# A per-channel gate moved from a projection's weights to its results, and one branch's additions moved to VectorE

## The chip, the cores and the metric

The kernel runs on one core of one Trainium2 chip. The metric is device time in microseconds (us) of one execution; several executions are summarised by their median. TensorE does the matrix products into PSUM (8 banks of 128x512 float32), VectorE (DVE), ScalarE (ACT) and GpSimd (POOL) do the elementwise work, and SyncE (SP) issues nearly all DMAs. Each engine works through its own instructions in the order of its queue, and waits at the head of the queue for whatever the next instruction needs.

## What is computed

A decoder block on a sequence of 1024 rows with 1024 channels. An S5 branch and a stick-breaking attention branch are merged by sigmoid gates, projected by `w_o`, scaled by a modulation row `g1` and added to the input; a SwiGLU feed-forward part follows.

```python
y_a = s5_branch(...) @ w_a
y_b = stick_breaking_attention(q, k, v) @ w_b
merged = (sigmoid(gate_a) * y_a + sigmoid(gate_b) * y_b) @ w_o
x = x + g1 * merged                                  # g1: one value for each of 1024 channels
h = modulate(rmsnorm(x, norm2_g), sh2, sc2)
ffn = (silu(h @ w_ffn_gate) * (h @ w_ffn_up)) @ w_ffn_down
x = x + g2 * ffn
return rmsnorm(x, norm_f_g)
```

## The kernel before

Every float32 matrix operand is split into a high part (a copy rounded to the type `F32R`, on ScalarE) and a low part (the difference, on VectorE), and each product is made of three matmuls (`PRODUCTS`: high by high, high by low, low by high). A matmul here is 128x128 by 128x512. The stages follow one another; three of them matter.

`branch_b` (L954) is the attention branch's projection and the merge. Four groups of output channels (`c`), two blocks `m` in each and two halves `h` of the sequence make 16 results. For each: the pre-activation of the gate (`gt`) and the S5 side (`ma`) are loaded by SP (L975, L976), ScalarE takes the sigmoid (L977), TensorE makes 12 matmuls into one PSUM bank (L982), VectorE multiplies the bank by `gt` (L984), which frees the bank, then `ma` is added (L985: on VectorE for `h` = 1, on GpSimd for `h` = 0), and `split` makes the high part on ScalarE (L904) and the low part on VectorE (L905). `gt` and `ma` have six buffers each, so the loads of a later result wait for an earlier one to be split. Between the groups, `ada_row` builds `g1` as a row repeated on all partitions (L886 writes it), and `ada_cols` builds two small columns.

`attend_out` (L1000) is the output projection, the residual and the norm. `c` counts two halves of the output channels. For each half, four weight tiles of 128x1024 come through `weight` (L404): load by SP (L411), times `g1` on GpSimd (L416), high part on ScalarE (L418), low part on VectorE (L421). For each block of 128 rows `t` (8 of them), 24 matmuls (L1018) fill a bank of the pool `wo`, and VectorE adds it to the row tile `x1[t]` (L1021). In the second half (`c` = 1) the finished row goes on: to DRAM (L1024), squared with a sum on ScalarE (L1030), the reciprocal root in seven small instructions (`rstd`, L449 to L460), scaled into the tile `xh` (L1032), and, for each odd `t`, two rows' `xh` are transposed on TensorE into four banks `tq` (L1040) and moved out by ScalarE (L1046, even `kk`) and VectorE (L1044, odd `kk`). `xh` is a tile of a pool `ot` with 3 buffers, except for `t` = 3 and 7, where it is the one buffer `row` of another pool. That buffer is the one that `g1` lies in: `g1` is last read by L416.

`ffn` (L1054) begins with `pieces` (L990), sums and splits of the transposed rows (L437, L439, L440), of which seven sets are needed before `gate_up`'s matmuls (L1137) can run without a break. The first two sets need rows 0 to 511 only (`t` up to 3); the others need all rows.

PSUM is handed over between `branch_b` and `attend_out`: the 16 results of `branch_b` go round 8 banks, and the three banks of `wo` are banks 1, 2 and 3. The 15th result of `branch_b` lies in bank 1 and the 16th in bank 2.

What sets the order: except for some pinned places, the order of the instructions in each engine's queue is written out by a scheduler ahead of time, from a model of the time that each takes; on the chip the order is fixed. A tile's buffer is given to its next user when all readers of the old tile are done.

Of the kernel before, what the change touches and what calls it, by code (L numbers as in the profile page):

```python
# [9 lines left out]
F32 = mybir.dt.float32  # L10
# [3 lines left out]
ALU = mybir.AluOpType  # L14
# [320 lines left out]
P = 128  # L335
# [56 lines left out]
class Block:  # L392
# [8 lines left out]
        return self.tc.tile_pool(name=name, bufs=bufs, space=space)  # L401


    def weight(self, src, scale=None, lo_eng=None, hi_eng=None, first=None, ring=None):  # L404

        nc = self.nc
        pool, ht, lt, spool, stag, sbufs = ring or self.next_ring()
        st = spool.tile([P, 1024], F32, name=stag, bufs=sbufs)
        h = pool.tile([P, 1024], F32R, name=ht)
        l = pool.tile([P, 1024], F32R, name=lt)  # L410
        ld = nc.sync.dma_start(out=st.rearrange("p (a b) -> p a b", b=src.shape[-1]) if len(src.shape) == 3 else st, in_=src)  # L411
        if first is not None:
            self.after(ld, first)
        if scale is not None:
            sv = st.rearrange("p (a b) -> p a b", b=src.shape[-1]) if len(src.shape) == 3 else st
            nc.gpsimd.tensor_tensor(sv, sv, scale, ALU.mult)  # L416
        if hi_eng is None:
            nc.scalar.copy(h, st)  # L418
        else:
            hi_eng.tensor_scalar(h, st, 1.0, 0.0, ALU.mult, ALU.add)  # L420
        (lo_eng or nc.vector).tensor_tensor(l, st, h.bitcast(F32), ALU.subtract)  # L421
        return h, l
# [531 lines left out]
    def branch_b(self, ops, const, tp, pa, spare, g1):  # L954
        nc, i = self.nc, self.i
# [3 lines left out]
        for c in range(4):  # L959
# [7 lines left out]
            for m in (2 * c, 2 * c + 1):  # L967
                wm = [t[:, :, P * (m % 2):P * (m % 2) + P] for t in w]
                for h in range(2):
                    s = slice(512 * h, 512 * h + 512)  # L970
                    if spare:
                        gt, ma = spare.pop(0)
                    else:
                        gt, ma = (tp.tile([P, 512], F32, name=n, bufs=6) for n in ("gb", "ma"))
                    nc.sync.dma_start(out=gt, in_=self.gD[1, P * m:P * m + P, s])  # L975
                    nc.sync.dma_start(out=ma, in_=self.nD[P * m:P * m + P, s])  # L976
                    self.after(nc.scalar.activation(gt, gt, AF.Sigmoid), self.last_exp)  # L977
                    ps = pa.tile([P, 512], F32)
                    j = 0
                    for k in range(4):  # L980
                        for a, b in PRODUCTS:
                            nc.tensor.matmul(ps, lhsT=wm[a][:, k], rhs=ops[k][b][:, s], start=(j == 0), stop=(j == 11))  # L982
                            j += 1
                    nc.vector.tensor_tensor(gt, ps, gt, ALU.mult)  # L984
                    (nc.vector if h else nc.gpsimd).tensor_tensor(gt, gt, ma, ALU.add)  # L985
                    self.split(mg[h][m][:, 0], mg[h][m][:, 1], gt)
        return mg

# [11 lines left out]
    def attend_out(self, mg, g1, const, tp, pp, tpp):  # L1000
# [4 lines left out]
        x1, xhs = [], []  # L1005
        for c in range(2):
            cs = slice(512 * c, 512 * c + 512)
            gc = g1[:, cs].unsqueeze(1).broadcast_to([P, 2, 512])
            ws = [self.w3(self.weight(src[:, 2 * a:2 * a + 2, cs], scale=gc), 512) for a in range(4)]
            for t in range(KT if c == 0 else 0):  # L1010
                x1.append(self.X.tile([P, 1024], F32, name="x1"))
                nc.sync.dma_start(out=x1[t], in_=x_v[:, t])
            for t in range(KT):
                ps = pp.tile([P, 512], F32, name="wo")
                j = 0
                for k in range(KT):
                    for a, b in PRODUCTS:
                        nc.tensor.matmul(ps, lhsT=mg[t // 4][k][:, a, P * (t % 4):P * (t % 4) + P], rhs=ws[k // 2][b][:, k % 2],  # L1018
                                         start=(j == 0), stop=(j == 23))
                        j += 1  # L1020
                nc.vector.tensor_tensor(x1[t][:, cs], ps, x1[t][:, cs], ALU.add)  # L1021
                if c == 0:
                    continue
                nc.sync.dma_start(out=self.xD[P * t:P * t + P], in_=x1[t])  # L1024
                if t % 4 == 0:
                    f = [[self.F.tile([P, 2, 512], F32, name=f"f{y}") for _ in range(2)] for y in range(2)]
                xh = self.rp.tile([P, 1024], F32, name="row") if t % 4 == 3 else tp.tile([P, 1024], F32, name="xh")
                xhs.append(xh)
                ss = const.tile([P, 1], F32, name="ss2", bufs=2)
                nc.scalar.activation(xh, x1[t], AF.Square, accum_out=ss)  # L1030
# [388 lines left out]
```

## Time and profile before

| | |
|---|---|
| median of 3 runs | 1570.67 us (1568.31 to 1572.18) |
| the profiled execution | 1567.69 us |
| its span, first to last instruction | 1566.0 us |
| TensorE busy | 1420.6 us (91%) |
| VectorE busy | 1076.0 us (69%) |
| GpSimd busy | 820.9 us (52%) |
| ScalarE busy | 615.5 us (39%) |
| mean granted TensorE clock | 0.965 |

The profile shows each instruction with its start and duration, and in brackets the idle time of its engine just before it and what ended that idle time. "issue" is idle time for which the profile shows no wait. The chain of waits is followed back from the end: each piece is the work that released the next one. The granted clock is a share of 2.4 GHz: 1.00 is that level and 0.50 is 1.2 GHz. A busy share is not a limit by itself; where it matters is which engine or wait ends last in a stage.

### The profile page before, as it was taken

Reading aid. Unit: us, or ns where it says so; the run is one execution under the profiler, and the core shown is the slowest. Engines: PE = TensorE matmul, PEld = TensorE weight load, DVE = VectorE, ACT = ScalarE, POOL = GpSimd, SP = SyncE. Lnnn points to the kernel's source line nnn. Section 1 sums busy time; section 2 is a strip of 40 time slices with the busy share of each in tenths; the row PEclk is TensorE's granted clock in tenths of the full one; section 3 lists DMA queues with packets and bytes.
Section 4 is the critical chain, followed back from the end, with each engine's and each line's share of the span. In section 5 each row is a group of like instructions: output and inputs, shape, how many; then the busy total and the mean of one; then the engine's idle time right before and its main releaser. Section 6 shows DMA issues by size and latency. Waiting matters only on the chain.

```text
span 1566.0 us, 18381 instructions
## 1 busy us (share of the span) xinstructions
PE 1420.6 (91%) x6578; PEld 1113.9 (71%) x6578; DVE 1076.0 (69%) x1309; ACT 615.5 (39%) x792; POOL 820.9 (52%) x643
## 2 busy tenths in 40 slices
PE   4898889799999889888799879999999998999995
PEld 2697767678765556556688668888888887788774
DVE  5548777543567687775733797666665667999998
ACT  5431111352465656564314643332223332443323
POOL 2488694010345455632430445544555469797795
PEclk9899999999999999999899989999999999999998
DMA  8456675635423233326443413333333238445422
GB/s 284 160 139 180 178 194 172 178 117 160 142 96 115 70 107 115 108 88 203 133 162 119 125 53 101 101 101 107 110 108 109 72 128 303 149 154 148 121 60 108
DMA packets 180451, 210.46 MB, mean 134 GB/s; under 512 B 28612, under 2 KB 121896, under 8 KB 180360
## 3 DMA queue, kind: packets, MB, share of 16 engines
q1 hardware_dynamic: 169288, 201.29, 40.8%
q10 hardware_dynamic: 11072, 8.00, 1.8%
q8 instruction: 52, 0.85, 0.2%
q14 instruction: 39, 0.32, 0.1%
HBM read 159.18 MB, written 48.89 MB: 133 GB/s over the span
## 4 chain that ended last, share of the span: by engine, by line
PE 26%; DVE 10%; issue 7%; POOL 6%; DMA 2%; ACT 1%; SPq 0%; DVEq 0%; POOLq 0%; ACTq 0%
PE tq L1137 10%; PE wo L1137 8%; PE wo L1018 5%; PE gu L1137 3%; POOL pb L1197 1%; POOL pa L1190 1%; DVE f L1221 1%; DMA pa<-in_w_ffn_down_dram 1%; POOL wb L1219 1%; DVE pb L1242 1%; DVE x L1242 1%; POOL x L1197 1%; DVE f L1217 1%; DVE wl L1217 1%; DVE ft L437 1%
## 5 line engine op out<-in xcount | busy, mean ns | idle before, releaser
L437 POOL TENSOR_TENSOR ws<-wb 128x1024 f32<-128x1024 f32 x29 | 73.2, 2526 | 105.8 <-DVE wl L440 59.9
L769 POOL TENSOR_SCALAR wh<-ws 128x1024 fp32r<-128x1024 f32 (+1 forms) x40 | 38.6, 964 | 122.6 <-DVE ws L768 88.5
L421 POOL TENSOR_TENSOR wl<-ws,wh 128x1024 fp32r<-128x1024 f32 x14 | 38.2, 2734 | 115.2 <-ACT wh L418 105.7
L437 POOL TENSOR_TENSOR wgs<-wb 128x1024 f32<-128x1024 f32 x15 | 37.9, 2526 | 103.5 <-DVE x L440 36.8
L770 DVE TENSOR_TENSOR wl<-ws,wh 128x1024 fp32r<-128x1024 f32 (+1 forms) x40 | 62.0, 1551 | 36.8 <-POOL wh L769 36.7
L780 POOL TENSOR_TENSOR wa<-wa,wb 128x1024 f32<-128x1024 f32 (+2 forms) x32 | 69.0, 2157 | 32.5 <-DMA wb<-cD 28.5
L802 ACT ACTIVATE wa<-wa 128x1024 f32<-128x1024 f32 (+1 forms) x40 | 38.9, 972 | 82.0 <-DVE wa L801 76.1
L801 DVE TENSOR_TENSOR wa<-wa,acc 128x512 f32<-128x512 f32 (+1 forms) x80 | 46.8, 623 | 34.2 <-POOL wa L780 34.2
L870 DVE SCALAR_TENSOR_TENSOR acc<-aw,cond,acc 128x512 f32<-128x512 f32 x56 | 54.7, 979 | 18.0 <-DMA aw<-in_w_ada_dram 17.4
L1190 POOL TENSOR_TENSOR pa<-pa,row 128x1024 f32<-128x1024 f32 x22 | 66.0, 3023 | 1.9 <-DMA pa<-in_w_ffn_down_dram 1.9
L768 DVE SCALAR_TENSOR_TENSOR ws<-wa,ws 128x1024 f32<-128x1024 f32 (+1 forms) x40 | 52.2, 1304 | 15.7 <-ACT ws L767 15.7
L1128 POOL TENSOR_TENSOR f<-f,f 128x512 f32<-128x512 f32 x30 | 49.1, 1661 | 26.0 <-DVE f L1118 17.5
L700 PE MATMUL acc<-wh,upto 128*128 128x512 f32 (+1 forms) x80 | 32.7, 408 | 28.9 <-DVE wa L801 26.6
L765 ACT ACTIVATE ws<-wa 128x1024 f32<-128x1024 f32 (+1 forms) x40 | 38.9, 974 | 35.6 <-DVE wa L762 35.0
L418 ACT CAST wh<-ws 128x1024 fp32r<-128x1024 f32 x28 | 29.2, 1047 | 55.9 <-PE wo L1018 30.7
L1219 POOL TENSOR_TENSOR wb<-pa 128x512 f32<-128x512 f32 x23 | 40.2, 1755 | 15.7 <-DVE wxl L1217 5.5
L1117 ACT ACTIVATE f<-f 128x1024 f32<-128x1024 f32 x22 | 23.3, 1061 | 57.4 <-DVE f L1157 30.3
L700 PE MATMUL z<-q,k 64*128 64x512 f32 (+3 forms) x192 | 41.8, 526 | 2.6 <-DVE wa L762 1.7
L700 PEld LDWEIGHTS acc<-wh,upto 128*128 128x128 f32 x80 | 15.5, 193 | 40.0 <-issue 29.3
L1128 POOL TENSOR_TENSOR f<-f 128x512 f32<-128x512 f32 x20 | 42.1, 2126 | 0.0
L1236 PE MATMUL wo<-f,f 128*128 128x512 f32 x132 | 40.6, 389 | 0.0
L700 PE MATMUL mm<-wa,V 128*64 128x512 f32 (+3 forms) x192 | 39.8, 507 | 0.4 <-ACT wa L802 0.4
(816 smaller groups left out, 4854.0 us busy)
## 6 DMA issues: line engine op xcount, KB each, us to landing
aw<-in_w_ada_dram SPq DMA_DIRECT2D x32, 512.0 KB
wb<-cD SPq DMA_DIRECT2D x32, 512.0 KB
hD<-f SPq DMA_DIRECT2D x30, 512.0 KB
ws<-in_w_in_dram SPq DMA_DIRECT2D x23, 512.0 KB
wb<-in_w_ffn_gate_dram SPq DMA_DIRECT2D x44, 256.0 KB
wb<-in_w_ffn_up_dram SPq DMA_DIRECT2D x44, 256.0 KB
pa<-in_w_ffn_down_dram SPq DMA_DIRECT2D x22, 512.0 KB
wb<-hD SPq DMA_DIRECT2D x40, 256.0 KB
```

The lines of the kernel that those rows point to most:

```text
L437: (add or nc.gpsimd).tensor_tensor(st, a, b, op)
L700: return self.tc.keep_in_program_order(self.nc.tensor.matmul(*args, **kw))
L768: nc.vector.scalar_tensor_tensor(st, a, 0.0, st, ALU.max, ALU.add)
L770: nc.vector.tensor_tensor(lt, st, ht.bitcast(F32), ALU.subtract)
L780: nc.gpsimd.tensor_tensor(a[:, :, o], a[:, :, o], g.behind[:, :, old], ALU.subtract)
L801: nc.vector.tensor_tensor(a[:, x, 0:f], a[:, x, 0:f], r[:, x, 0:f], ALU.subtract)
L870: nc.vector.scalar_tensor_tensor(acc, w[:, j], cj, acc, ALU.mult, ALU.add)
L1018: nc.tensor.matmul(ps, lhsT=mg[t // 4][k][:, a, P * (t % 4):P * (t % 4) + P], rhs=ws[k // 2][b][:, k % 2], start=(j == 0), stop=(j == 23))
L1128: nc.gpsimd.tensor_tensor(o, a, b, op)
L1137: self.nc.tensor.matmul(ps, lhsT=w[x][:, q, k], rhs=self.B[i](y, k), start=(j == 0), stop=(j == 11))
L1190: nc.gpsimd.tensor_tensor(w, w, g2, ALU.mult)
L1219: last_sum = nc.gpsimd.tensor_tensor(st[:, R], u, W[p][b[0]][:, 512 * b[1]:512 * b[1] + 512], SIGN_B[i])
```

## The change

`weight` loses its `scale` parameter and the GpSimd multiplication with it. In `attend_out` the result of each `t` and `c` is multiplied by `g1` as it leaves PSUM, into the first 512 columns of an `xh` tile, and a second instruction adds that to `x1[t]`. So `xh` is taken for both halves `c`, always from the pool `ot` with its 3 buffers; `row` is no longer one of its buffers, and `g1` stays in it until the end of `attend_out`. In `branch_b` all 16 additions are on VectorE.

```diff
-    def weight(self, src, scale=None, lo_eng=None, hi_eng=None, first=None, ring=None):
+    def weight(self, src, lo_eng=None, hi_eng=None, first=None, ring=None):
...
-        if scale is not None:
-            sv = st.rearrange("p (a b) -> p a b", b=src.shape[-1]) if len(src.shape) == 3 else st
-            nc.gpsimd.tensor_tensor(sv, sv, scale, ALU.mult)
...
                     nc.vector.tensor_tensor(gt, ps, gt, ALU.mult)
-                    (nc.vector if h else nc.gpsimd).tensor_tensor(gt, gt, ma, ALU.add)
+                    nc.vector.tensor_tensor(gt, gt, ma, ALU.add)
                     self.split(mg[h][m][:, 0], mg[h][m][:, 1], gt)
...
-            gc = g1[:, cs].unsqueeze(1).broadcast_to([P, 2, 512])
-            ws = [self.w3(self.weight(src[:, 2 * a:2 * a + 2, cs], scale=gc), 512) for a in range(4)]
+            ws = [self.w3(self.weight(src[:, 2 * a:2 * a + 2, cs]), 512) for a in range(4)]
...
-                nc.vector.tensor_tensor(x1[t][:, cs], ps, x1[t][:, cs], ALU.add)
+                xh = tp.tile([P, 1024], F32, name="xh")
+                nc.vector.tensor_tensor(xh[:, 0:512], ps, g1[:, cs], ALU.mult)
+                nc.vector.tensor_tensor(x1[t][:, cs], xh[:, 0:512], x1[t][:, cs], ALU.add)
                 if c == 0:
                     continue
...
-                xh = self.rp.tile([P, 1024], F32, name="row") if t % 4 == 3 else tp.tile([P, 1024], F32, name="xh")
                 xhs.append(xh)
```

## Rows read from the trace of the kernel before

**Rows 1.** The page's line of busy time, share of the span and number of instructions of each engine.

```profile
PE 1420.6 (91%) x6578; PEld 1113.9 (71%) x6578; DVE 1076.0 (69%) x1309; ACT 615.5 (39%) x792; POOL 820.9 (52%) x643
```

**Rows 2.** Busy time of the engines in stretches of the span (start:end, length, then PE, PEld, DVE, ACT and POOL with their instructions, the granted clock, the DMA share and GB/s).

```profile
747.00:775.00 28.00, 27.45 (x131) 22.89 (x129) 19.02 (x23) 11.70 (x18) 11.12 (x6) 0.94 0.43 134
775.00:784.00 9.00, 0.17 (x1) 0.20 (x2) 8.52 (x9) 2.21 (x3) 5.92 (x3) 0.66 0.14 55
784.00:829.00 45.00, 45.00 (x190) 37.05 (x191) 14.66 (x15) 7.67 (x8) 10.76 (x5) 0.95 0.38 141
829.00:868.00 39.00, 39.00 (x185) 32.18 (x184) 14.18 (x38) 20.52 (x39) 2.40 (x1) 1.00 0.45 149
868.00:895.00 27.00, 22.75 (x112) 17.83 (x110) 26.33 (x30) 15.97 (x24) 16.71 (x5) 1.00 0.31 99
895.00:923.00 28.00, 17.02 (x63) 12.37 (x63) 24.15 (x16) 13.14 (x16) 15.98 (x6) 0.78 0.19 55
```

**Rows 3.** The waits between 772 and 784 us: who waited for whom, us in total, times, the longest.

```profile
PE wo L1018 <- DVE gb L984: 9.4, 1, 9.4
```

**Rows 4.** The chain that ended last, from 769 us into the output projection (start, us, what).

```profile
769.92 2.98 DMA gb<-gD
...
776.19 1.27 POOL gb L985
...
778.14 2.62 DVE pa L905
...
781.36 0.60 DVE gb L984
781.96 1.13 DVE wb L421
783.09 0.61 DVE gb L984
...
783.84 60.29 PE wo L1018 x256
```

**Rows 5.** TensorE's matmuls in order of time: the last of `branch_b`, the first of `attend_out`, the one at which full speed is back, and the last of `attend_out`.

```profile
774.06 0.39 PE L982 MATMUL bb<-oh,wl 128*128 128x512 f32 x1
783.84 0.77 PE L1018 MATMUL wo<-wh,pa 128*128 128x512 f32 x1 [9.39 <-DVE gb L984]
...
788.16 0.40 PE L1018 MATMUL wo<-wl,pa 128*128 128x512 f32 x1
...
877.44 0.39 PE L1018 MATMUL wo<-wh,pb 128*128 128x512 f32 x1
```

**Rows 6.** VectorE's instructions in order of time: a low part of `branch_b`, and four of the additions in the second half of `attend_out` (`t` = 3, 5, 6, 7).

```profile
751.46 0.68 DVE L905 TENSOR_TENSOR pb<-gb,pb 128x512 fp32r<-128x512 f32 x1
...
852.37 0.69 DVE L1021 TENSOR_TENSOR x<-wo,x 128x512 f32<-128x512 f32 x1 [2.51 <-PE wo L1018]
...
865.15 0.69 DVE L1021 TENSOR_TENSOR x<-wo,x 128x512 f32<-128x512 f32 x1 [3.24 <-PE wo L1018]
...
872.63 0.68 DVE L1021 TENSOR_TENSOR x<-wo,x 128x512 f32<-128x512 f32 x1
...
883.91 0.68 DVE L1021 TENSOR_TENSOR x<-wo,x 128x512 f32<-128x512 f32 x1
```

**Rows 7.** GpSimd's instructions in order of time, three of those between 760 and 780 us.

```profile
762.17 2.40 POOL L416 TENSOR_TENSOR ws<-ws,row 128x1024 f32<-128x1024 f32 x1 [7.15 <-issue]
764.53 1.28 POOL L985 TENSOR_TENSOR gb<-gb,ma 128x512 f32<-128x512 f32 x1
...
777.41 2.79 POOL L416 TENSOR_TENSOR ws<-ws,row 128x1024 f32<-128x1024 f32 x1
```

**Rows 8.** The waits of SP's queue between 720 and 900 us (who waited for whom, us in total, times, the longest).

```profile
SPq L976 <- POOL gb L985: 11.0, 4, 6.1
...
SPq L1012 <- DVE pb L905: 2.3, 1, 2.3
```

**Rows 9.** The instructions of L416 on the tiles `ws` (ns: shortest, median, longest; first and last start).

```profile
L416 POOL TENSOR_TENSOR ws<-ws,row x7: 2388/2668/3135, 748.2 to 807.7; 128x1024 f32<-128x1024 f32 x7
```

**Rows 10.** The same for L985, on the two engines.

```profile
L985 DVE TENSOR_TENSOR gb<-gb,ma x7: 684/1066/2446, 739.2 to 785.5; 128x512 f32<-128x512 f32 x7
L985 POOL TENSOR_TENSOR gb<-gb,ma x7: 1265/1300/2206, 739.3 to 782.1; 128x512 f32<-128x512 f32 x7
```

**Rows 11.** TensorE alone in short stretches: length, busy time, granted clock, DMA share, GB/s.

```profile
778.00:780.00 2.00, 0.00 (x0) 0.50 0.00 0
...
892.00:896.00 4.00, 1.16 (x6) 1.00 0.94 262
```

**Rows 12.** TensorE's transposes in order of time: the last of blocks `t` = 0 and 1, four of block 3 (its first half), the last of the pair 2 and 3, and the second half of `t` = 4 and 5.

```profile
856.48 0.38 PE L1040 MATMUL tq<-ident,xh 128*128 128x128 f32 x2
...
862.68 0.60 PE L1040 MATMUL tq<-ident,row 128*128 128x128 f32 x4
...
869.12 0.27 PE L1040 MATMUL tq<-ident,row 128*128 128x128 f32 x1
...
881.08 1.03 PE L1040 MATMUL tq<-ident,xh 128*128 128x128 f32 x8
```

**Rows 13.** ScalarE's instruction that scales block `t` = 3 into `xh` (the tile `row`).

```profile
857.55 1.15 ACT L1032 ACTIVATE row<-x,ry 128x1024 f32<-128x1024 f32 x1 [2.18 <-DVE ry L460]
```

**Rows 14.** The chain that ended last, a piece of it after the last block's transposes.

```profile
899.66 5.94 DVE ft L437 x2
```

## The prediction

> **What bounds the kernel now.** I began with the busy shares: TensorE is at work for 91% of the span [rows 1], so a change in elementwise work pays only where TensorE stands or where its next work comes late. Then I cut the stages around the change into stretches [rows 2]. The reader should see three regimes. Up to 775 us TensorE is full and VectorE has a third of its time free. From 775 to 784 TensorE does nothing and VectorE is full: a gap between two stages. From 784 to 868 TensorE is full again and VectorE works about a third of the time. After 868 the roles change: VectorE is busy 26.3 of 27 us and then 24.2 of 28, while TensorE waits for its products. I call 868 to 923 the tail.
>
> The view of waits names the gap: 9.4 us in which the first matmul of the output projection waits for the multiplication L984 that empties the last bank of the attention branch [rows 3]. The chain of waits shows why that is late although its matmuls ended at 774.45 [rows 4, 5]: a load of a gate lands at 772.9, GpSimd adds one result (1.27 us), ScalarE splits it, VectorE takes 2.62 us for a low part that takes 0.68 elsewhere [rows 6], and only behind that stand the last two L984, with a weight's low part of 1.13 between them. VectorE's queue is in order, so the two full banks wait behind a result that is going round by GpSimd. The list of GpSimd's work shows the same earlier: L416 starts at 762.17 and the addition L985 queued behind it only at 764.53 [rows 7]. Buffers of the gates come free late for that reason, and the loads with them: SP's queue stood 11.0 us before loads of `ma` for L985 on GpSimd [rows 8].
>
> **The change, part by part.**
>
> The weights' scaling. Eight L416 of about 2.67 us, 21 us of GpSimd, go [rows 9]. GpSimd bounds nothing between 747 and 868 [rows 2], so this is worth only what it unblocks: GpSimd's queue, and VectorE's low part from 2.62 back to about 0.68 [rows 4, 6]. The weights need one step less between load and high part; after the gap TensorE never waits for a weight, so that is worth nothing.
>
> The additions. Eight go from GpSimd (1.30) to VectorE. Their price there: between 0.60, the spacing of two such instructions without GpSimd beside them, and 2.45, the longest now [rows 6, 10]. I take 0.60, as nothing is left on GpSimd in this stage: 4.8 us, less than the 9 us that VectorE has free in 747 to 775 [rows 2]. Per result VectorE then has three instructions (L984, L985, L905), 1.8 us, beside TensorE's 12 matmuls, 2.7 us. So it keeps up, the splits follow at once, gates are loaded earlier, and what remains after the last matmul is one L984 of 0.69 and some 0.2 of hand-over.
>
> Term 1, the gap: 9.4 becomes 0.9, a gain of **8.5**. Bounds: 2.7 if only the GpSimd step (1.27 instead of 0.60 with two hand-overs, 0.8) and the slowed low part (1.9) go; 9.4 if the whole gap does.
>
> Term 2, the clock. The granted clock fell to 0.50, the level of 1.2 GHz, at about 778, after 3.5 us of standing [rows 11]. The first 10 matmuls took 4.32 us (783.84 to 788.16 [rows 5]); the chain's 256 pieces in 60.29 us [rows 4] leave (60.29 - 4.32) / 246 = 0.2275 for a later one, so the lost time is 2.05. Between 892 and 896 TensorE worked 1.16 us of 4 and kept 1.00 [rows 11]. With a gap of 0.9 I take the whole **2.05** as gained; bounds 0 and 2.05.
>
> The new multiplication takes the place of L1021: PSUM and one SBUF operand, as now, 0.68 to 0.69 even at 872.63 with GpSimd at work [rows 6], so it frees a bank no later. The new addition has both operands in SBUF. In the first half and for `t` = 0 to 4 of the second, VectorE has 30 of 45 and 25 of 39 us free [rows 2]: hidden, cost nothing; the cover is that idle time, and each addition would cost its 0.60 without it. In the tail VectorE has nothing free.
>
> Term 3, the tail's extra work. Blocks `t` = 6 and 7 get one addition each. Block 5 comes in too: its multiplication writes the buffer of block 2, whose last transpose ends at 869.4 (869.12 + 0.27 [rows 12]), so 865.15 [rows 6] becomes 869.4, inside the tail, with 0.60 and an addition. For an addition beside GpSimd (busy 33 of these 55 us [rows 2]) the nearest row is the median on VectorE in the attention branch, 1.07 [rows 10]. 0.60 + 3 x 1.07 = **3.8** lost. Bounds 1.2 (two at 0.60, block 5 out of it) and 0.60 + 3 x 2.45 = 8.0.
>
> A DVE instruction with two SBUF operands is where the Trainium skill speaks against this change: SBUF — State Buffer, section Who interferes with whom, says that it contends with a GpSimd instruction that reads SBUF, and that the loser blocks for the whole instruction. By that rule each addition would stand for a GpSimd instruction, and term 3 would be its upper bound; the 2.45 of the slowest addition agrees, the median of 1.07 says that most meet none.
>
> Term 4, three buffers instead of four. Block 3's multiplication needs block 0's buffer, read until 856.86 (856.48 + 0.38 [rows 12]); its addition now starts at 852.37 [rows 6], so the block is 4.5 later, plus 0.7 for the second instruction. Its scaling ended at 858.70 [rows 13] and would end at 863.9; its first transposes stand at 862.68 in TensorE's queue [rows 12]. TensorE would stand for **1.2**. Bounds 0, where the queue puts other matmuls there, and 5.5, a whole slot of 24 matmuls, where the transposes fall behind the next block.
>
> SP's queue: no load is added; the loads of `x1`, now behind the last low part of the branch [rows 8], come earlier. Block 7's multiplication needs block 4's buffer, read until 882.1 [rows 12], before 883.91 [rows 6]: nothing.
>
> **Sum**: - 8.5 - 2.05 + 3.8 + 1.2 = -5.5. The profiled execution, 1567.69 (span 1566.0 and 1.7 around it), would become 1562.2. It lies 3.0 below the median of the runs, so for a median I take 1570.67 - 5.5 = **1565.1**.
>
> **The rivals.**
>
> *Three buffers cost a whole slot.* The transposes of blocks 2 and 3 fall behind the next block's matmuls: term 4 is 5.5, sum -1.3, 1569.4. For it: transposes already stand about one slot of 24 matmuls apart in the queue [rows 12]. Against it: 9 us lie between block 3's scaling (858.70) and its last transposes (869.12).
>
> *The port between VectorE and GpSimd.* Each addition of the tail stands for a whole GpSimd instruction: term 3 is 8.0, sum -1.4, 1569.3. For it: 2.45 was seen [rows 10], and GpSimd is busy 33 of 55 us. Against it: the median. This is what the rule of the Trainium skill's page SBUF — State Buffer would do here.
>
> *The gap stays half.* The change does not do what the additions suggest: VectorE's new order keeps the last L984 behind a weight's low part whose load is late, so only 2.7 of the gap goes and the clock falls all the same: -2.7 + 3.8 + 1.2 = +2.3, 1573.0. For it: a low part stands between the last two L984 now [rows 4]. Against it: its weight would be loaded and split earlier.
>
> *Slower: VectorE stands for `xh`.* If the order puts the multiplications of blocks 3, 5 and 7 ahead of work that could pass them, VectorE waits for transposes in its own queue: 5.5 for block 3, 4.2 for block 5 (865.15 to 869.4), 4.3 for block 7 (matmuls done 877.8 [rows 5], buffer free 882.1). 14.0 instead of 1.2: -8.5 - 2.05 + 3.8 + 14.0 = +7.2, 1577.9. It decides from the point where the waits exceed 10. Against it: the tail has other VectorE work until about 895, and an order made from these dependencies would place it first.
>
> **How the numbers follow.** A measurement of this kernel can tell about 0.3%, 4.7 us, from no change. The forecast (-5.5, its own range -10 to -4) has 0.50; the first three rivals, all within 4.7, have 0.16, 0.09 and 0.11; the slower one 0.14. The forecast lies just past the bound, so a small error of term 3 or 4 moves it into "same". The range: below, terms 1 and 2 at their ends with term 3 at 1.2 and term 4 at 0 give -10.2, and 2.4 for the spread of runs below the median: 1558. Above, the half gap's 1573.0 and 1.5 to 2 of spread: 1575. That leaves out the slower rival and little else.
>
> **What would show it.** Term 1: the wait of the first L1018 under 2 us, and no GpSimd work between 735 and 840. Term 2: the first L1018 0.39 long, clock 1.00 throughout. Term 3: three additions after the last block's start with durations of 0.7 to 2.5, and the tail's sums (L437), 5.94 for two now [rows 14], unchanged. Term 4: idle time of TensorE before a transpose of block 3. The forecast is wrong if the gap stays over 5 us, if VectorE's additions wait for L1040, or if the stretch from the projection's last matmul to unbroken L1137 (45 us now) grows by more than 10.

## The result, and the profile after

Before and after ran 20 times each on the same chips: 1567.32 us before (1562.2 to 1572.18), 1572.84 after (1569.02 to 1577.62). The ratio is **1.0037**, with a 95% interval of [1.0026, 1.0048]: the change costs some 5.8 us. Forecast was a gain of 5.5. The profiled execution of after took 1576.08, with a span of 1574.4 and a mean granted clock of 0.958.

The busy shares of after, against [rows 1]: GpSimd has 34 us less and VectorE 12 more, as meant.

```profile
PE 1432.7 (91%) x6578; PEld 1123.3 (71%) x6578; DVE 1088.1 (69%) x1333; ACT 616.1 (39%) x792; POOL 786.9 (50%) x627
```

The stretches of [rows 2], and one more (the columns are the same):

```profile
747.00:775.00 28.00, 28.00 (x134) 23.63 (x133) 20.27 (x33) 11.37 (x18) 0.00 (x0) 0.94 0.49 161
775.00:784.00 9.00, 5.36 (x20) 4.02 (x19) 8.38 (x12) 3.75 (x5) 0.00 (x0) 0.89 0.32 114
784.00:829.00 45.00, 45.00 (x197) 37.22 (x196) 16.58 (x21) 6.01 (x6) 0.00 (x0) 0.98 0.40 144
829.00:868.00 39.00, 39.00 (x186) 32.27 (x185) 16.95 (x37) 19.05 (x35) 2.39 (x1) 1.00 0.36 118
868.00:895.00 27.00, 20.14 (x83) 15.09 (x81) 21.00 (x25) 13.65 (x22) 10.94 (x4) 0.87 0.17 59
895.00:923.00 28.00, 23.11 (x76) 16.98 (x76) 23.06 (x22) 11.59 (x17) 17.09 (x6) 0.70 0.38 113
923.00:950.00 27.00, 19.98 (x77) 15.91 (x77) 24.28 (x24) 14.05 (x17) 8.04 (x3) 0.81 0.20 59
```

The last stretch in the kernel before:

```profile
923.00:950.00 27.00, 27.00 (x109) 22.15 (x110) 23.95 (x26) 11.24 (x13) 7.69 (x3) 0.91 0.22 65
```

The gap at 775 has become smaller (TensorE 5.36 us busy of 9 instead of 0.17). The tail has become longer: in 895 to 923 the granted clock is 0.70 instead of 0.78, and TensorE still stands idle for 7 us of the 27 from 923, where before it ran without a break.

To compare executions that reach this point at different times, I cut each profile at three places: the end of `branch_b`'s last matmul, the first and the last matmul of the output projection, and the start of `gate_up`'s unbroken matmuls. The first piece is the **gap**, then the **projection**, then the **tail**; "last transposes" is the start of the last L1037 (L1040 before) after the projection's end.

| one profile each, us | gap | projection | tail | sum | last transposes |
|---|---|---|---|---|---|
| before | 9.39 | 94.00 | 45.01 | 148.40 | 20.76 |
| after | 3.64 | 92.61 | 56.90 | 153.15 | 33.39 |

So 5.75 were gained in the gap, 1.4 in the projection, and 11.9 lost in the tail: +4.75. The spans differ by 8.4; of the other 3.65, 3.3 lie ahead of `branch_b`'s end, and 2.2 of these ahead of its first matmul, where both kernels issue the same work in the same order. The end of its last matmul came at 772.9 to 778.0 in the profiles below, whatever the kernel (767.9 in one, psum7).

One profile's gap has to be read with care, because it also depends on when TensorE ends `branch_b`. Up to the projection, after and four kernels below (half3, psum7, four_buffers, three_control) have the same instructions in the same order on VectorE and ScalarE and none on GpSimd, and their gaps are 2.3 to 6.0. The time from `branch_b`'s first matmul to the projection's first is steadier: 59.4 to 60.9 in these five, against 65.6 in before and 64.0 in ring3, a kernel below that is the same as before up to there. I give this time as **first to first** where the gap alone would mislead; differences of some 1.6 us in it show nothing.

**The gap.** ScalarE in order of time, between 761 and 764 us:

```profile
761.85 0.63 ACT L974 ACTIVATE gb<-gb 128x512 f32<-128x512 f32 x1 [3.23 <-DMA gb<-gD]
763.20 0.63 ACT L974 ACTIVATE gb<-gb 128x512 f32<-128x512 f32 x1 [0.71 <-DMA gb<-gD]
763.73 0.60 ACT L901 CAST pa<-gb 128x512 fp32r<-128x512 f32 x1
```

VectorE, from there to its last product of `branch_b` (answers to [rows 6]):

```profile
764.37 0.69 DVE L902 TENSOR_TENSOR pa<-gb,pa 128x512 fp32r<-128x512 f32 x1 [3.69 <-ACT pa L901]
764.98 0.68 DVE L981 TENSOR_TENSOR gb<-bb,gb 128x512 f32<-128x512 f32 x1
765.70 0.69 DVE L982 TENSOR_TENSOR gb<-gb,ma 128x512 f32<-128x512 f32 x1
767.07 0.69 DVE L902 TENSOR_TENSOR pb<-gb,pb 128x512 fp32r<-128x512 f32 x1 [0.69 <-ACT pb L901]
...
769.78 0.69 DVE L902 TENSOR_TENSOR pa<-gb,pa 128x512 fp32r<-128x512 f32 x1 [0.69 <-ACT pa L901]
...
779.40 1.22 DVE L418 TENSOR_TENSOR wb<-ws,wb 128x1024 fp32r<-128x1024 f32 x1
780.54 0.68 DVE L981 TENSOR_TENSOR gb<-bb,gb 128x512 f32<-128x512 f32 x1
```

TensorE, the last matmul of `branch_b` and the first of the projection (answers to [rows 5]):

```profile
777.35 0.39 PE L979 MATMUL bb<-oh,wl 128*128 128x512 f32 x1
781.37 0.47 PE L1014 MATMUL wo<-wh,pa 128*128 128x512 f32 x1 [3.64 <-DVE gb L981]
```

The reader should see a stall and why it is not made up in time. ScalarE waits at the head of its queue for two gates to land, and a cast that has been ready since 760.7 (an addition of VectorE started at 759.99) stands behind the two sigmoids. VectorE waits 3.69 us for that cast. In the laps that follow one result takes 2.7 us on VectorE, because its order is product, addition, wait for the cast, low part (764.37, 767.07, 769.78 are 2.7 apart). TensorE makes a result in 2.7 too, so the lag stays. From 773.6 on VectorE has no such wait left and a result takes it 2.0, but low parts of weights stand between (1.22 at 772.50 and at 779.40), and the last product starts 2.8 us after TensorE's last matmul has ended. GpSimd has nothing to do here any more, and the waits of SP's queue for it [rows 8] are gone; the loads of gates (L972) and of S5 sides (L973) wait for VectorE instead, 18.2 us in all between 720 and 905, where before it was 11.7 beside the 11.0 for GpSimd.

**The tail.** VectorE in order of time (answers to [rows 6]):

```profile
854.57 0.68 DVE L1018 TENSOR_TENSOR xh<-wo,row 128x512 f32<-128x512 f32 x1
...
872.89 0.68 DVE L1018 TENSOR_TENSOR xh<-wo,row 128x512 f32<-128x512 f32 x1
...
873.94 0.68 DVE L1018 TENSOR_TENSOR xh<-wo,row 128x512 f32<-128x512 f32 x1
...
876.68 0.68 DVE L1019 TENSOR_TENSOR x<-xh,x 128x512 f32<-128x512 f32 x1
...
881.72 2.85 DVE L1019 TENSOR_TENSOR x<-xh,x 128x512 f32<-128x512 f32 x1
...
894.80 0.68 DVE L1018 TENSOR_TENSOR xh<-wo,row 128x512 f32<-128x512 f32 x1
...
897.11 0.68 DVE L1019 TENSOR_TENSOR x<-xh,x 128x512 f32<-128x512 f32 x1
...
899.13 2.04 DVE L457 TENSOR_TENSOR ry<-ry,ra 128x1 f32<-128x1 f32 x1
```

GpSimd, two of its instructions beside them:

```profile
880.78 3.23 POOL L434 TENSOR_TENSOR ws<-wb 128x1024 f32<-128x1024 f32 x1
...
897.14 4.01 POOL L434 TENSOR_TENSOR ws<-wb 128x1024 f32<-128x1024 f32 x1 [1.42 <-DVE x L437]
```

TensorE's transposes of blocks 2 and 3 (865.89, 871.11), 4 and 5 (890.44), 6 and 7 (904.69), the last ones of each pair (answers to [rows 12]):

```profile
865.89 0.60 PE L1037 MATMUL tq<-ident,xh 128*128 128x128 f32 x4
871.11 1.03 PE L1037 MATMUL tq<-ident,xh 128*128 128x128 f32 x8
...
890.44 1.80 PE L1037 MATMUL tq<-ident,xh 128*128 128x128 f32 x8 [0.33 <-ACT f L1043]
895.53 5.49 PE L1134 MATMUL wo<-pa,x 128*128 128x512 f32 x12 [3.29 <-DVE xh L1018]
...
904.69 3.10 PE L1037 MATMUL tq<-ident,xh 128*128 128x128 f32 x12 [1.63 <-ACT xh L1029]
```

The multiplications of blocks 3, 5, 6 and 7 are the four at 854.57, 872.89, 873.94 and 894.80. Block 7's bank was full at 874, and it is emptied at 894.80, 21 us later, when block 4's transposes have left their buffer; the addition of block 7 came at 883.91 before [rows 6]. The chain of waits of after now runs through these multiplications:

```profile
871.27 0.23 PE tq L1037 x2
871.53 1.45 DVE f L1041 x3
872.98 0.60 DVE xh L1018
...
891.80 0.45 PE tq L1037 x2
892.41 1.02 issue
893.44 1.44 DVE f L1041 x3
894.88 0.60 DVE xh L1018
...
908.44 6.41 DVE ft L434 x2
```

The last row is the piece of [rows 14], 8.8 us later than before, though the projection started 2.5 earlier.

### The profile page after: what moved, and what is told of

It is laid out like the page before. It is cut to its first block, busy times and chain, and to the rows that moved or that the text cites. A ratio compares the mean times of both kernels' runs of the same rounds, so it can differ in the third digit from the quotient of the medians.

```text
span 1574.4 us, 18388 instructions
## 1 busy us (share of the span) xinstructions
PE 1432.7 (91%) x6578; PEld 1123.3 (71%) x6578; DVE 1088.1 (69%) x1333; ACT 616.1 (39%) x792; POOL 786.9 (50%) x627
## 4 chain that ended last, share of the span: by engine, by line
PE 32%; DVE 9%; issue 5%; POOL 4%; DMA 3%; ACT 2%; SPq 0%; DVEq 0%; ACTq 0%; POOLq 0%
PE tq L1134 10%; PE wo L1134 8%; PE wo L1014 6%; PE tq L1233 3%; PE gu L1134 3%; PE wo L1233 2%; POOL pb L1194 1%; DMA gb<-gD 1%; DMA pa<-in_w_ffn_down_dram 1%; DVE f L1218 1%; DVE x L1239 1%; PE gu L1233 1%; DVE ft L434 1%; DVE pb L1239 1%; POOL x L1194 1%
## 5 line engine op out<-in xcount | busy, mean ns | idle before, releaser
L767 DVE TENSOR_TENSOR wl<-ws,wh 128x1024 fp32r<-128x1024 f32 (+1 forms) x40 | 65.7, 1641 | 36.8 <-POOL wh L766 36.8
```

What stands on the lines that cost most here:

```text
L767: nc.vector.tensor_tensor(lt, st, ht.bitcast(F32), ALU.subtract)
```

## Experiments

All ratios are to the kernel before, from runs on the same chip (5 to 12 of each kernel). Gap, projection, tail and last transposes are in us and from one profile each.

**adds_only.** Kernel before, with the additions alone moved.

```diff
-                    (nc.vector if h else nc.gpsimd).tensor_tensor(gt, gt, ma, ALU.add)
+                    nc.vector.tensor_tensor(gt, gt, ma, ALU.add)
```


> Only the 16 additions are on VectorE; weights still scaled on GpSimd, xh as before. Theory (three buffers lengthen the tail, the gap gain is from branch_b): gap 9.4 falls to some 4 to 6 us, tail (last projection matmul to unbroken L1137) stays 45 +- 1, so 3 to 7 us faster than before. Rival (the gap gain came from the removed scaling on GpSimd): gap stays 8 to 9.4, time within 1 us of before.

Measured: 1565.9, 0.9985 [0.9969, 1.0001]: no gain that is clear of the noise, where 3 to 7 us were expected. Gap 6.9, projection 93.9, tail 42.7. The gap is 2.5 shorter, but TensorE also took longer over `branch_b` (57.3 us, against 56.2 in before and 54.6 in ring3), and first to first is 64.1, between the 65.6 and 64.0 of those two. So no gain of the additions alone is shown at the gap. The 2.4 in the tail were not expected (see the end).

**gate_only.** Kernel after, with the additions as before (the diff above, reversed).

> The gate on the results, additions on GpSimd for h = 0 as before. Theory: tail as in the changed kernel, 55 to 58 us, gap between 4 and 8 because GpSimd no longer scales but still adds: 5 to 10 us slower than before. Rival (additions on VectorE are what lengthens the tail): tail 45 to 48, faster than before by the gap.

Measured: 1572.34, 1.0025 [1.0012, 1.0039]. Gap 2.2 (4 to 8 was expected), first to first 58.3, projection 91.0, tail 56.5. It is the missing L416 that shortens the gap, by at least as much as in after, and the gate's new place brings the whole loss of the tail.

**ring3.** Kernel before, with all `xh` from the three buffers.

```diff
-                xh = self.rp.tile([P, 1024], F32, name="row") if t % 4 == 3 else tp.tile([P, 1024], F32, name="xh")
+                xh = tp.tile([P, 1024], F32, name="xh")
```


> The kernel before, with xh always from the three buffers of its pool (taken at the square, as before; no new instruction, weights scaled as before). Theory: blocks 3, 5 and 7 wait for transposes: tail 50 to 55 instead of 45, 5 to 9 us slower than before. Rival (the tail grew by the extra VectorE instructions and GpSimd's port): tail 45 to 46, same time as before.

Measured: 1570.33, 1.0016 [1.0001, 1.0031]. Tail 48.5, less than the 50 to 55 expected; last transposes 27.6 after the projection's end instead of 20.8. Here `xh` is still taken only at the square, so no PSUM bank waits for it.

**half3.** Kernel after, but the second half's product goes into the first half of `g1` (no longer needed there), and `xh` is taken at the square.

```diff
-                xh = tp.tile([P, 1024], F32, name="xh")
-                nc.vector.tensor_tensor(xh[:, 0:512], ps, g1[:, cs], ALU.mult)
-                nc.vector.tensor_tensor(x1[t][:, cs], xh[:, 0:512], x1[t][:, cs], ALU.add)
+                sc = tp.tile([P, 1024], F32, name="xh")[:, 0:512] if c == 0 else g1[:, 0:512]
+                nc.vector.tensor_tensor(sc, ps, g1[:, cs], ALU.mult)
+                nc.vector.tensor_tensor(x1[t][:, cs], sc, x1[t][:, cs], ALU.add)
```


> The changed kernel, but in the second half the product goes to the first half of g1 (no longer needed there), and xh is taken only at the square, from the same three buffers. Theory, if it is the early taking of xh that counts: tail 46 to 50, 3 to 6 us faster than before; if three buffers alone count: tail as in ring3. Rival (extra VectorE instructions): tail 55 to 57 as in the changed kernel, 5 us slower than before.

Measured: 1567.96, 1.0004 [0.999, 1.0019]. Gap 3.3, tail 52.5, last transposes 30.0. Taking `xh` later gives back 4.4 us of the tail; the tail came out between the two theories.

**psum7.** Kernel after, with the product written back to its PSUM bank, `xh` taken at the square, and `row` as block 7's `xh`.

```diff
-                xh = tp.tile([P, 1024], F32, name="xh")
-                nc.vector.tensor_tensor(xh[:, 0:512], ps, g1[:, cs], ALU.mult)
-                nc.vector.tensor_tensor(x1[t][:, cs], xh[:, 0:512], x1[t][:, cs], ALU.add)
+                nc.vector.tensor_tensor(ps, ps, g1[:, cs], ALU.mult)
+                nc.vector.tensor_tensor(x1[t][:, cs], ps, x1[t][:, cs], ALU.add)
...
+                xh = self.rp.tile([P, 1024], F32, name="row") if t == 7 else tp.tile([P, 1024], F32, name="xh")
```


> The changed kernel with the product written back to the PSUM bank, so that xh is taken only at the square, and block 7's xh in the tile of g1 (free by then); the others from three buffers. Theory (early taking 4.5, three buffers 3.5, additions 3.9 of the tail's 11.8): early taking gone, part of the ring's price gone: tail 49 to 52, gap 3 to 4, 1 to 4 us faster than before. Rival (a bank is now held for two instructions and TensorE waits for it, or the additions alone make the tail): tail 54 or more, slower than before.

Measured: 1566.01, 0.9985 [0.9966, 1.0004]. Gap 6.0 (3 to 4 was expected; first to first 60.6), tail 50.4, last transposes 29.5. One more buffer for the last block alone brings 2.1 against half3, and the place of the product has changed with it, so this run decides nothing by itself.

**hybrid.** Gate on the results in the first half only; the second half's weights are scaled on GpSimd as before, and its `xh` are as before.

```diff
-            ws = [self.w3(self.weight(src[:, 2 * a:2 * a + 2, cs], scale=gc), 512) for a in range(4)]
+            ws = [self.w3(self.weight(src[:, 2 * a:2 * a + 2, cs], scale=gc if c else None), 512) for a in range(4)]
...
+                if c == 0:
+                    sc = tp.tile([P, 1024], F32, name="xh")[:, 0:512]
+                    nc.vector.tensor_tensor(sc, ps, g1[:, cs], ALU.mult)
+                    nc.vector.tensor_tensor(x1[t][:, cs], sc, x1[t][:, cs], ALU.add)
+                    continue
                 nc.vector.tensor_tensor(x1[t][:, cs], ps, x1[t][:, cs], ALU.add)
-                if c == 0:
-                    continue
```


> The kernel before with the gate on the results in the first half of the channels only; the second half's weights are scaled on GpSimd as before, xh as before with four buffers, additions of the branch as before. Theory (in the first half the new instructions are hidden; the tail's loss comes from the second half alone; the gap gain comes from the scaling that no longer stands in GpSimd's queue): gap about 2, tail 45, 7 to 10 us faster than before. Rival (the remaining scalings on GpSimd still hold up the additions, or VectorE's extra work in the first half shows): gap 5 or more, 0 to 4 us faster.

Measured: 1561.66, 0.9953 [0.9937, 0.997]. Gap 4.0 (about 2 was expected), first to first 60.1, tail 45.3, last transposes 20.8. The gain in the gap stays and the loss in the tail is gone: the change's two halves are a gain and a loss.

**hybrid_vec.** hybrid, with all additions on VectorE (the diff of adds_only).

> As hybrid, with all additions of the branch on VectorE. Theory (after the stall near 761 us VectorE has no slack, so each added instruction delays the last multiplication): gap 3 to 4, 1 to 2 us slower than hybrid. Rival (the additions on VectorE help as in adds_only): gap under 2, as fast as hybrid or faster.

Measured: 1560.36, 0.994 [0.9923, 0.9957]. Gap 5.1, first to first 61.3, tail 42.1. The gap is no shorter; the tail is, as in adds_only. The expected loss of 1 to 2 us did not come.

**hybrid_7.** hybrid, with seven buffers for `gb` and `ma` instead of six (`bufs=7`).

> As hybrid, with seven instead of six buffers each for the loads of the gates and of the other branch. Theory (VectorE's stall of 4 to 5 us near 761 comes from gates that are loaded late for want of a buffer): stall under 3, gap under 2, 0 to 2 us faster than hybrid. Rival (the stall comes from the order on ScalarE or the time of a load): stall and gap unchanged, same time.

Measured: 1561.72, 0.9957 [0.9936, 0.9977]. Gap 2.9, first to first 59.1, but VectorE's stall is still there: 5.01 us before the low part at 761.55, where hybrid has 4.77. One more buffer does not shorten it.

**hybrid_order.** hybrid_vec, with each sigmoid ordered on ScalarE behind the cast of the result four earlier. It then can't stand in front of that cast.

```diff
-                    self.after(nc.scalar.activation(gt, gt, AF.Sigmoid), self.last_exp)
+                    sg = nc.scalar.activation(gt, gt, AF.Sigmoid)
+                    self.after(sg, self.last_exp)
+                    if len(casts) >= 4:
+                        self.after(sg, casts[-4])
...
-                    self.split(mg[h][m][:, 0], mg[h][m][:, 1], gt)
+                    casts.append(self.split(mg[h][m][:, 0], mg[h][m][:, 1], gt))
```


> As hybrid_vec, with one rule of order more: a gate's sigmoid stands in ScalarE's queue behind the high part of the result four before it, so that a late load no longer holds up a result that is ready. Theory (what is left of the gap, 5.1, comes from the 3.6 us in which VectorE waits near 761 for a high part that stands behind sigmoids waiting for loads): the stall falls under 1.5, gap under 2, 2 to 4 us faster than hybrid_vec. Rival (VectorE is simply behind, or the loads are late all the same): gap 4 to 5, same time.

Measured: 1558.31, 0.9934 [0.9914, 0.9955]: the shortest of all, ahead of both kernels, though its interval overlaps hybrid_vec's. In its profile VectorE no longer waits more than 0.7 us for a cast (758.54 to 766.66, in the same laps of 2.7), and the wait of TensorE at the gap is this row (us in total, times, longest):

```profile
PE wo L1022 <- DVE gb L988: 1.1, 1, 1.1
```

First to first is 57.2, against 60.4 to 61.3 in hybrid_vec and the three kernels below that have its order up to the projection (late_op, early_four, early_ring; stalls of 2.92 to 3.59). So the stall's part of the gap is some 3 to 4 us.

**four_buffers and three_control.** Kernel after with a pool of four `xh` buffers. To make room, a weight pool (`wx`) is opened only after the projection; the control has that and three buffers, and differs from four_buffers in this line alone.

```diff
-                with self.pool("ot", 3, side="right") as tp:
+                with self.pool("ot", 4, side="right") as tp:
```


> The changed kernel with four buffers for xh in place of three. Room for the fourth is made by opening the pool wx only after the projection; the second half's second weight tile uses the ring wb in its place. Theory (the ring of three, taken early, costs 8 us of the tail, the additions the other 3.9): tail 47 to 50 instead of 56.9, block 7's product no longer waits for the transposes of blocks 4 and 5, time 3 to 7 us below three_control. Rival (the ring counts for little, the tail is long for its additions and their order): tail 54 or more, same time as three_control.

> The control of four_buffers: the same place of wx and the same weight ring, three buffers. Theory and rival alike: tail 55 to 58, time as the changed kernel within 3 us, 3 to 8 us slower than before.

Measured: 1572.73, 1.0029 [1.0011, 1.0046] against 1573.51, 1.0038 [1.0022, 1.0054]. With four buffers the last transposes come 6.7 us earlier (28.0 against 34.7), but between them and the end of the tail 4.5 us are lost again (28.2 against 23.7), and the tail is only 2.2 shorter (56.2, 58.3). My theory that the fourth buffer is worth most of the loss failed here. Where the 4.5 went can be read on VectorE. Until 20 us after the last transposes the two kernels run alike. Then four_buffers has a weight's low part and a sum between two low parts that three_control makes in a row, and the second of these takes until 925.7, beside a GpSimd instruction from 921.34 to 924.60. VectorE of four_buffers:

```profile
920.04 1.22 DVE L437 TENSOR_TENSOR wl<-ws,wh 128x1024 fp32r<-128x1024 f32 x1
...
922.32 4.50 DVE L437 TENSOR_TENSOR x<-ft,x 128x1024 fp32r<-128x1024 f32 x2
```

VectorE of three_control:

```profile
925.07 2.42 DVE L437 TENSOR_TENSOR x<-ft,x 128x1024 fp32r<-128x1024 f32 x2
```

By these rows it is the order written for four_buffers that took the gain back; what it would gain in the other order was not tried. The next three differ from one to the next in one thing of the code; the written order still follows from it.

**late_op.** hybrid_vec, with one more VectorE instruction per block of the second half, which leaves the value as it is.

```diff
                 nc.vector.tensor_tensor(x1[t][:, cs], ps, x1[t][:, cs], ALU.add)
+                nc.vector.tensor_tensor(x1[t][:, cs], x1[t][:, cs], x1[t][:, cs], ALU.max)
```


> hybrid_vec with one more VectorE instruction for each block of the second half, behind the residual's addition: the maximum of x1's half with itself (the value does not change, both operands in SBUF). xh and its buffers as in hybrid_vec. This is the extra instruction alone. Hybrid_vec's tail (end of the output projection to gate_up's unbroken matmuls) was 42.1 us, its ratio to the kernel before 0.994. Theory 'the extra instructions themselves are the smaller part': tail 45 to 47 (the 3.8 of the prediction's term 3), ratio about 0.9965. Rival 'the instruction, with the order that it brings, is most of it': tail 50 or more, ratio about 0.999 or above.

**early_four.** hybrid_vec, with the second half in after's two steps (a copy stands for the multiplication), and with `row` for blocks 3 and 7 as in before.

```diff
-                nc.vector.tensor_tensor(x1[t][:, cs], ps, x1[t][:, cs], ALU.add)
+                xh = self.rp.tile([P, 1024], F32, name="row") if t % 4 == 3 else tp.tile([P, 1024], F32, name="xh")
+                nc.vector.tensor_copy(xh[:, 0:512], ps)
+                nc.vector.tensor_tensor(x1[t][:, cs], xh[:, 0:512], x1[t][:, cs], ALU.add)
```


> hybrid_vec, but in the second half each PSUM bank is copied by VectorE into the first 512 columns of an xh tile that is taken at once, and a second instruction adds that to x1: the second half's pattern of the changed kernel (the copy in the multiplication's place; the weights of this half are still scaled on GpSimd), but with the buffers of the kernel before, the one buffer row for blocks 3 and 7 and three for the others. Theory 'the smaller number of buffers is the larger part': tail 45 to 48, last transposes no more than 24 us after the projection's end, ratio about 0.9965 to 0.998. Rival 'two steps with early taking cost it whatever the buffers': tail 52 or more, ratio about 1.000.

**early_ring.** early_four, with all `xh` from the three buffers (the diff of ring3).

> early_four with all blocks' xh from the pool of three buffers, as in the changed kernel: with hybrid_vec's first half and additions. Theory: the tail of the changed kernel comes back, 54 to 57 us (56.9 there), last transposes about 33 after the projection's end, ratio about 1.002; the difference to early_four is the price of the three buffers once the product is taken early (6 to 10 us). Rival 'the scaled weights matter, not the buffers': tail below 50.

| each adds to the one above | median | ratio and interval | gap | projection | tail | last transposes |
|---|---|---|---|---|---|---|
| hybrid_vec | 1560.36 | 0.994 [0.9923, 0.9957] | 5.1 | 93.3 | 42.05 | 20.75 |
| late_op | 1563.14 | 0.9968 [0.9947, 0.9989] | 2.9 | 92.0 | 45.18 | 24.41 |
| early_four | 1563.1 | 0.9971 [0.9953, 0.9989] | 2.7 | 92.0 | 45.27 | 24.42 |
| early_ring | 1571.18 | 1.002 [1.0002, 1.0038] | 4.8 | 92.4 | 54.88 | 33.04 |

The three rows of early_four, early_ring and late_op stand against hybrid_vec's from an earlier set of runs on another chip, each by its ratio to the kernel before; the intervals of hybrid_vec and late_op overlap. This is what four_buffers could not tell. The extra instruction costs 3.1 in the tail, with the order that comes with it. Taking `xh` early costs nothing more (0.1) while there are four buffers; late_op and early_four have the same order on VectorE, ScalarE and GpSimd in the tail. The step from four buffers to three, with its order, costs 9.6 in the tail and 8.1 in the medians of one chip.

The piece up to the last transposes repeats closely: it is 20.75 to 20.89 in the six kernels whose second half is that of before (before, adds_only, hybrid, hybrid_vec, hybrid_7, hybrid_order), and 33.30 in gate_only beside 33.39 in after. The steps of 3.7, 0.0 and 8.6 in that column stand clear of this.

Block 7's copy out of its bank and the transposes show how the buffers do it. VectorE of early_four, block 7's copy:

```profile
875.35 0.68 DVE L1027 COPY row<-wo 128x512 f32<-128x512 f32 x1
```

TensorE of early_four, transposes of blocks 2 and 3 (854.96, the last at 860.97), the last eight of 4 and 5 (872.01) and the first four of 6 and 7:

```profile
854.96 0.60 PE L1044 MATMUL tq<-ident,row 128*128 128x128 f32 x4
...
860.97 0.27 PE L1044 MATMUL tq<-ident,row 128*128 128x128 f32 x1
...
872.01 1.03 PE L1044 MATMUL tq<-ident,xh 128*128 128x128 f32 x8
...
888.36 1.11 PE L1044 MATMUL tq<-ident,xh 128*128 128x128 f32 x4 [7.60 <-ACT xh L1036]
```

VectorE of early_ring, block 7's copy:

```profile
892.43 0.68 DVE L1027 COPY xh<-wo 128x512 f32<-128x512 f32 x1
```

TensorE of early_ring, the same groups (863.74 and 868.96; 888.33; 900.04):

```profile
863.74 0.60 PE L1044 MATMUL tq<-ident,xh 128*128 128x128 f32 x4
...
868.96 1.03 PE L1044 MATMUL tq<-ident,xh 128*128 128x128 f32 x8
...
888.33 2.05 PE L1044 MATMUL tq<-ident,xh 128*128 128x128 f32 x8 [1.78 <-ACT f L1050]
...
900.04 0.66 PE L1044 MATMUL tq<-ident,xh 128*128 128x128 f32 x4 [1.39 <-ACT xh L1036]
```

The projection ends 3.1 us later in early_ring (872.1 against 869.0). Measured from that end, the transposes of 2 and 3 fall 5 to 6 us back, the last of 4 and 5 13 us, and block 7's copy, which needs block 4's buffer, 14 us. In early_four TensorE stood 7.60 us for block 6 anyway; the first transposes of 6 and 7 are 8.6 later in early_ring, and 9.6 are left at the end of the tail.

## Why the prediction was wrong

**Term 1, the gap: right in part, too large.** 8.5 was forecast, 5.75 came in the profile (first to first 3 to 5 us less than in before and ring3), between my bounds; the sign that I had named, a wait under 2 us, did not come (3.64). Taking L416 off GpSimd's queue is what shortens the gap (gate_only 9.4 to 2.2); of the additions no gain is shown there (first to first 64.1 in adds_only). The sentence that failed is that VectorE "keeps up, the splits follow at once, gates are loaded earlier". I added up VectorE's instructions, 1.8 us per result, and left out its wait for the cast inside each lap, which makes it 2.7 behind a stall: no slack. Nor did I look at ScalarE's queue, where a sigmoid waits for its load ahead of a cast that could run. The trace of the kernel before shows it at the same place:

```profile
762.84 1.26 ACT L977 ACTIVATE gb<-gb 128x512 f32<-128x512 f32 x2 [5.00 <-DMA gb<-gD]
765.84 0.62 ACT L904 CAST pa<-gb 128x512 fp32r<-128x512 f32 x1 [1.74 <-POOL gb L985]
```

The two sigmoids ended at 764.10, and GpSimd held this cast back for 1.74 us more; so by this trace only that much of the wait was GpSimd's. hybrid_order takes the sigmoids from before the cast and has a gap of 1.1, near the 0.9 of the forecast.

**Term 2, the clock: 2.05 forecast, about 0.4 came.** After a gap of 3.6 the first matmul took 0.47 instead of 0.77 [rows 5], but the next ones slowed. From 781.37 to the twelfth matmul at 785.56 there are 4.19 us; 11 at 0.2275 are 2.50, so 1.69 is lost, against 2.05. In these 4.2 us the granted clock was 0.60, before 0.51 in the first 4.3. The clock that I wanted came where the gap was shorter: gate_only, after 2.20 us of standing, kept 1.00 from its first matmul of the projection to its last. The projection of after is 1.4 shorter, but it also holds 34 of the 64 transposes instead of 40: six moved out of it into the tail, which is no gain.

**Term 3, the tail's extra instructions: right in size.** 3.8 forecast, 3.1 in late_op, with the order that came with them. Three additions do lie after the last block's start (0.68, 2.85, 0.68). By the Trainium skill, SBUF — State Buffer, section Who interferes with whom, the port pair that VectorE and GpSimd share is an exclusive lock, and the one that comes second blocks until the other's instruction is done; the 2.85 agrees (it began 0.94 behind a GpSimd instruction of 3.23, and ended 0.56 after it). But one addition of three met it, so term 3 did not become the 8.0 of that rival. My price for each, the median of 1.07, was misread: of the eight additions on VectorE in the kernel before, three met none (0.68 to 0.69), and the other five (0.70, 1.07, 1.31, 1.35, 2.45) all began behind a GpSimd instruction and ended 0.55 after it. So the median did not say that most meet none, and that 3.8 came out near 3.1 is in part luck.

**Term 4, three buffers: the step that failed.** 1.2 forecast, with 5.5 as its upper bound; early_ring against early_four shows **9.6**, 8.6 of it up to the last transposes. I priced block 3's delay alone, as one idle piece of TensorE, and then compared the other blocks with the release times of the kernel before. "Block 7's multiplication needs block 4's buffer, read until 882.1 [rows 12], before 883.91 [rows 6]: nothing" uses a time that the delay of blocks 3 and 5 had already moved: in after block 4's buffer was read until 892.24 (890.44 + 1.80). With three buffers the waits are in series: block 3 waits for block 0's transposes, so the pair 2 and 3 is transposed late; block 5 waits for block 2's transposes, so the pair 4 and 5 is late; block 7 waits for block 4's. I knew each of these links and added no two of them. What I had said would prove me wrong, a tail longer by over 10, is what came: 11.9.

**The sum, with what the runs showed.** -5.75 (gap), -1.4 (projection), +3.1 (instructions) and +8.8 for what is left of the tail's 11.9, which the 9.6 of the buffers nearly is: +4.75 in the profiles, and +5.8 by the ratio. The parts add best up to the last transposes: of the 12.6 between before (20.8) and after (33.4), late_op's step is 3.7, early_four's 0.0 and early_ring's 8.6, and 0.3 are left. What does not add lies behind the last transposes (24.3 in before, 21.3 in hybrid_vec, 21.8 in early_ring, 23.5 in after): hybrid_vec is 3.0 below before there (see the end), and after is 1.7 above early_ring for a reason I have not shown.

**The rivals.** The one nearest to what came is the slower one, which priced the waits of blocks 3, 5 and 7 one after the other: +7.2, with a chance of 0.14. Its places were right. Its mechanism was not wholly so: VectorE itself stood for transposes only for 3.65 us at 853.20 and 3.08 at 906.54 (its longest wait, 7.38 before 870.17, was for a weight's cast); the order put its instructions where their data came. What waited was the full banks, and at 895 TensorE behind them (3.29). "Three buffers cost a whole slot" had the right cause at half the price. It priced that one delay alone: the transposes of blocks 2 and 3 ended 5.2 us later than before, counted from the projection's start (872.14, 869.39). The gap that "stays half" did not come. Its 1573.0 lies beside the measured 1572.84, and 1572.84 lies within my range of 1558 to 1575, but both by luck: the range was drawn to 1575 for this rival's cause.

## What to carry to other kernels

When a change takes buffers from a ring, or makes a tile be taken earlier, walk the ring block by block with the new times: each late release delays the next taker, and a delay that looks hidden for one block is added to by the next. Time an engine's lap with the waits inside it, not the sum of its instructions: VectorE, with a third of its time free, had no slack after a stall. And try a change's halves one by one; here the gate on the results is a gain in the first half (0.9953) and a loss in the second.

## What the runs showed that I had not expected

A tiny VectorE instruction can stand for GpSimd. L457, with 128x1 operands, takes 0.16; the one at 899.13 took 2.04 and ended with the GpSimd instruction that had run since 897.14 (901.17 and 901.15). It lies on the chain of waits, ahead of the last blocks' scaling. late_op and early_four have one of 2.12 and early_ring one of 2.04, each ending within 0.02 us of a GpSimd instruction. In before, all L460 on these tiles took 0.15 to 0.16; another 128x1 sum of that line, near the kernel's end, took 1.23 there and ended beside GpSimd in the same way (1557.71 and 1557.69).

Moving only `branch_b`'s additions shortened the tail, more than 80 us later, by 2.4 (adds_only) and 3.2 (hybrid_vec against hybrid), all of it behind the last transposes. Upstream I found no cause for that; the written order differs in the tail: two casts of `pieces` (L439) stand earlier on ScalarE and a weight's low part later on VectorE. That this order is the cause was argued from the orders, and not tried alone; four_buffers lost its 4.5 us where such a low part stood early.
